# A four-layer streaming encoder step on one core: the residual stream kept transposed, with the output weights as the stationary operand

## The chip, the cores and the metric

The kernel runs on one core of a Trainium2 chip. The metric is the device time of one execution in microseconds, as the median of several executions. TensorE (PE) multiplies matrices; VectorE (DVE), ScalarE (ACT) and GpSimd (POOL) work element by element; SyncE (SP) issues the transfers (DMAs) between memory and the on-chip buffer.

## The reference

One inference step of an encoder with four layers (kinds A, B, C, A) over 512 prompt rows and 64 sample rows of width 1024. Every layer is

```
z = rmsnorm(x, norm_g) @ w_in          # one input projection: mixer inputs and a gate
o = mixer(z)                           # A, B, C: three kinds of attention with RMSNorm on q and k
x = x + (o * silu(gate)) @ w_out       # the residual

def rmsnorm(x, g):
    y = x * rsqrt(mean(x * x, axis=-1) + 1e-6)
    return y * g
```

In every mixer q and k pass through an RMSNorm per head; in kind C the low-rank q, the KV latent and the rotary key too. v and the gate don't.

## The kernel before

The 576 rows (TOK: 512 prompt, 64 sample) stand in five token tiles (TT): four of 128 and one of 64 rows. Widths of 1024 are cut into KD = 8 pieces of 128. All matmuls of the projections are made in a split form: each fp32 operand is written as a high part and a low part (fp32r), and a product is the sum of three matmuls, high by high, high by low and low by high. The high part is a copy on ACT, the low part a subtraction on DVE or POOL.

**Projections by token tile** (`mm_tok`, L155 to L175). The stationary operand (loaded into the array by a weight load of its own) is a 128x128 piece of the transposed activations (`xT` or `oT`), the moving operand a piece of the weights, up to 512 columns wide. The result has tokens on the partitions. The 64 sample rows put their high and low parts side by side as one 128-wide stationary operand (two matmuls in place of three), and the two halves of the result are added by ACT and DVE (`lo`).

**Gates** (`gates`, L211 to L236). Here the weights are stationary and the activations move, in two halves of 288 tokens (HALF): the result has the channels on the partitions and tokens on the free axis. One half gate is 8 x 3 matmuls, ACT's tanh, a DVE product, and in A and B a POOL product into the attention's output.

**Output projection** (`out_proj`, L257 to L265). Two halves of 512 output columns; in each, the five token tiles by `mm_tok`; a DVE addition onto the residual tile `x[t]`. In the second half `after` stores the tile to memory and calls `norm` for it.

**Norm and transposes** (`norm`, L184 to L202). For a token tile: square sum (ACT), power -0.5 (`rstd`: DVE, POOL), multiplication by the factor and by the gain row (DVE), eight transposes on PE through the identity, and the high and low parts of the next layer's `xT` (ACT, DVE).

**Splitting the operand** (`split_o`, L250 to L254). Eight blocks of the gated attention output: the high part on ACT, the low part on POOL as two instructions (512 and 64 columns).

**Order.** The program is written layer by layer, with units of projection work interleaved by hand into the attention (`mix`). The order on each engine is then made by a scheduler from the dependencies, and is fixed when the program is built. PSUM has eight banks: three for projections (tag `mm`), two for scores (`s`), two for transposes (`t`), one for attention outputs (`o`). Weights pass through four staging buffers (`ws`) and eight pairs of split ones (`wh`, `wl`).

Of the kernel before, what the change touches and what calls it, by code (L numbers as in the profile page):

```python
# [9 lines left out]
F32 = mybir.dt.float32  # L10
F32R = mybir.dt.float32r
# [29 lines left out]
def encoder_step(ctx: ExitStack, tc: tile.TileContext, I, O):  # L41
# [17 lines left out]

    def ps_s():  # L60
        return ps.tile([128, 512], F32, tag="s", name="s", bufs=2)
# [38 lines left out]
    x = []  # L100
# [3 lines left out]
    def load_x(pool, src):  # L104
        x.clear()
        for t, (t0, tn) in enumerate(TT):
            xt = sb(D, f"x{t}", pool=pool)
            last = ld(xt[:tn], src[t0 : t0 + tn, :])
            x.append(xt)
        return last.ins  # L110

    def rstd(ss, tn, n, inv):
        r = sb(n, "nv", pool=tiny)[:tn]
        for lo, hi, f in inv if isinstance(inv, list) else [(0, n, inv)]:
            V.tensor_scalar(out=r[:, lo:hi], in0=ss[:, lo:hi], scalar1=f, scalar2=EPS, op0=ALU.mult, op1=ALU.add)  # L115
        G.tensor_tensor(out=r, in0=r, in1=bc(mhalf[:tn], tn, n), op=ALU.pow)  # L116
        return r
# [36 lines left out]
    def mm_tok(xT, nh, t0, tn, pieces, n, p=None, c0=0, w0=0):  # L154
# [17 lines left out]
        lo = sb(512, "lo", 1)[:64, :n]  # L172
# [11 lines left out]
    def norm(t, g, xT):  # L184
        t0, tn = TT[t]
        ss = sb(1, "nss", pool=tiny)[:tn]
        junk = sb(D, "sq", 2, dt=BF16)[:tn]
        S.activation(junk, x[t][:tn], AF.Square, accum_out=ss)
        r = rstd(ss, tn, 1, 1.0 / D)
        for hf in range(2):  # L190
            xs = rows_of(tn)
            cs = slice(hf * 512, hf * 512 + 512)
            V.scalar_tensor_tensor(out=xs[:tn], in0=x[t][:tn, cs], scalar=r, in1=g[:tn, cs], op0=ALU.mult, op1=ALU.mult)  # L193
            pt = v3(ps_t(), 128)
            for j in range(4):
                tr(pt[:, j, :], xs[:, j * 128 : j * 128 + 128])
            k0 = hf * 4
            l0 = lo_at(t0, TOK)
            hl_evac(xT[:, k0 : k0 + 4, t0 : t0 + tn], xT[:, k0 : k0 + 4, l0 : l0 + tn], pt[:, :, :tn])
            if tn == DEC:  # L200
                end = V.tensor_copy(xT[:, k0 : k0 + 4, 2 * TOK : WT], xT[:, k0 : k0 + 4, TOK : TOK + DEC].bitcast(F32))
        return end.ins if tn == DEC else None  # L202
# [8 lines left out]
    def gates(xT, w, c0, ogs, done=None):  # L211
        st = []

        def half(m, og, hf):
# [35 lines left out]
    def split_o(oT, b, src):  # L250
        S.activation(oT[:, b, :TOK], src, AF.Copy)  # L251
        for a, c in ((0, SEQ), (SEQ, TOK)):
            l0 = lo_at(a, TOK)
            G.tensor_tensor(out=oT[:, b, l0 : l0 + c - a], in0=src[:, a:c], in1=oT[:, b, a:c].bitcast(F32), op=ALU.subtract)  # L254

    def out_proj(w, oT, after):
        for nh in range(2):  # L257
            pieces = load_chunk(w, [(nh * 512, 512)])
            for t in range(len(TT)):
                t0, tn = TT[t]  # L260
# [11 lines left out]
    def layer_a(li, xT, first=None):  # L272
        w = I["a_w_in"][li]
        with tc.tile_pool(name=f"la{li}", bufs=1, reuse_waits="tile") as lp:
# [4 lines left out]
            def v_units(pp, pieces=None):  # L279
                st = [pieces] if pieces else []  # L280

                def unit(t, t0, tn):
# [6 lines left out]
                    p = mm_tok(xT, TOK, t0, tn, st[0], 512)  # L289
                    S.activation(vt[:tn, t, :], p, AF.Copy)  # L290
# [4 lines left out]
            def qk_units(pr):  # L295
                st = []

                def unit(t, t0, tn):
# [10 lines left out]
                    r = rstd(ss, tn, 4, 1.0 / 128)  # L309
# [114 lines left out]
            run(u[1:])  # L424
            for p in range(4):
# [649 lines left out]
```

## Time and profile before

| what | value |
|---|---|
| median of 3 runs | 1267.1 us (1267.1 to 1268.33) |
| the profiled execution's own time | 1270.64 us |
| its span on the core | 1268.7 us |
| PE busy | 1239.4 us, 7479 matmuls |
| DVE, ACT, POOL busy | 717.2, 646.9, 383.6 us |
| share of PE in the chain that ended last | 94% |

The span is the time from the program's first instruction to its last on the core; the execution's own time has 1.94 us more around it. Busy times of PE count a matmul with its latency, so consecutive matmuls overlap in them: the rate at which PE works is read from the distance between starts, or from the busy time of a whole stretch over its count.

### The profile page before, as it was taken

To read this page: it belongs to the slowest core of one execution; us is meant where nothing else is said; L and a number is where in the kernel's file an instruction comes from. 1 tells how busy PE (TensorE), PEld (TensorE's weight loads), DVE (VectorE), ACT (ScalarE), POOL (GpSimd) and SP (SyncE) were. 2 spreads that over 40 slices of the span, in tenths; PEclk is the share of its full clock that TensorE was granted. 3 is DMA by queue.
4 is the path that set the end of the run, shared out by engine and by line. 5 is a ranking of instruction groups with operands and counts; after the bars stand their busy time and mean duration, and the time that the engine had idled before them with its cause. 6 is when DMAs were issued, how large, how long until landed. Compare 5 with 4: busy or idle time off the path is not lost.

```text
span 1268.7 us, 21162 instructions
## 1 busy us (share of the span) xinstructions
PE 1239.4 (98%) x7479; PEld 1064.4 (84%) x7479; DVE 717.2 (57%) x1975; ACT 646.9 (51%) x1637; POOL 383.6 (30%) x488
## 2 busy tenths in 40 slices
PE   6999999999999999999999999999999999999998
PEld 4888888998889999778998887876788888889986
DVE  5166534733669888526577767685263656247332
ACT  4345443652447676514466767686243454435431
POOL 3322202223145351321275444541310322022150
PEclk9999999999999999999999999999999999999999
DMA  6432341442446232334131111112344323424322
GB/s 208 131 94 88 105 142 51 141 141 72 164 118 214 58 90 61 125 100 134 58 100 52 53 30 34 35 51 71 101 163 140 95 89 102 131 62 143 111 78 69
DMA packets 92889, 127.12 MB, mean 100 GB/s; under 512 B 10864, under 2 KB 64528, under 8 KB 92720
## 3 DMA queue, kind: packets, MB, share of 16 engines
q1 hardware_dynamic: 92784, 125.77, 31.7%
q8 instruction: 59, 0.97, 0.3%
q14 instruction: 46, 0.38, 0.1%
HBM read 105.81 MB, written 24.26 MB: 103 GB/s over the span
## 4 chain that ended last, share of the span: by engine, by line
PE 94%; DVE 2%; ACT 2%; DMA 1%; issue 1%; SPq 0%; POOL 0%; DVEq 0%; POOLq 0%; ACTq 0%
PE mm L163 16%; PE mm L165 16%; PE mm L164 16%; PE t L178 9%; PE mm L224 5%; PE mm L225 5%; PE mm L226 5%; PE mm L168 4%; PE mm L169 4%; PE o L379 3%; PE s L856 3%; PE o L866 2%; PE s L371 2%; PE o L593 1%; DMA x<-in_x 1%
## 5 line engine op out<-in xcount | busy, mean ns | idle before, releaser
L116 POOL TENSOR_TENSOR nv<-nv,mhalf 128x4 f32<-128x4 f32 (+7 forms) x147 | 152.6, 1043 | 424.2 <-DVE nv L115 409.3
L120 ACT ACTIVATE wh<-ws 128x512 fp32r<-128x512 f32 (+2 forms) x288 | 169.4, 616 | 113.5 <-PE mm L168 73.2
L163 PE MATMUL mm<-wh,T 128*128 128x512 f32 (+2 forms) x608 | 222.4, 371 | 1.2 <-DVE qs L515 1.0
L165 PE MATMUL mm<-wh,T 128*128 128x512 f32 (+2 forms) x608 | 223.5, 369 | 0.0
L164 PE MATMUL mm<-wl,T 128*128 128x512 f32 (+2 forms) x608 | 220.8, 368 | 1.4 <-DVE wl L121 1.4
L121 DVE TENSOR_TENSOR wl<-ws,wh 128x512 fp32r<-128x512 f32 (+2 forms) x252 | 170.3, 697 | 36.5 <-ACT wh L120 33.0
L224 PE MATMUL mm<-T,wh 128*128 128x288 f32 x512 | 155.8, 304 | 0.1
L225 PE MATMUL mm<-T,wh 128*128 128x288 f32 x512 | 152.9, 299 | 0.0
L226 PE MATMUL mm<-T,wl 128*128 128x288 f32 x512 | 152.8, 299 | 0.0
L163 PEld LDWEIGHTS mm<-wh,T 128*128 128x128 f32 x608 | 114.9, 189 | 17.6 <-DVE qs L515 1.2
L164 PEld LDWEIGHTS mm<-wl,T 128*128 128x128 f32 x608 | 114.8, 189 | 17.5 <-DVE wl L121 1.8
L165 PEld LDWEIGHTS mm<-wh,T 128*128 128x128 f32 x608 | 114.8, 189 | 16.7 <-DVE T L182 0.6
L163 PE MATMUL mm<-wh,oT 128*128 128x512 f32 x256 | 99.7, 398 | 2.5 <-ACT oT L251 1.9
L165 PE MATMUL mm<-wh,oT 128*128 128x512 f32 x256 | 100.3, 399 | 1.3 <-POOL oT L254 1.3
L164 PE MATMUL mm<-wl,oT 128*128 128x512 f32 x256 | 100.9, 396 | 0.0
L224 PEld LDWEIGHTS mm<-T,wh 128*128 128x128 f32 x512 | 96.2, 188 | 3.4 <-issue 1.9
L225 PEld LDWEIGHTS mm<-T,wh 128*128 128x128 f32 x512 | 96.2, 188 | 1.9 <-issue 1.8
L226 PEld LDWEIGHTS mm<-T,wl 128*128 128x128 f32 x512 | 96.1, 188 | 1.1 <-issue 1.1
L232 POOL TENSOR_TENSOR o<-o,sq 128x288 f32<-128x288 f32 x52 | 44.8, 862 | 162.2 <-DVE sq L230 90.0
L263 DVE TENSOR_TENSOR x<-mm,x 128x512 f32<-128x512 f32 x32 | 21.6, 690 | 118.8 <-PE mm L165 113.9
L178 PE MATMUL t<-ident,qs 128*128 128x128 f32 (+1 forms) x376 | 62.1, 277 | 13.1 <-DVE qs L193 10.3
L349 DVE CUSTOM_DVE_ANT_0 ex<-s,bias 128x128 f32<-128x128 f32 (+1 forms) x64 | 30.9, 486 | 61.8 <-PE s L371 55.4
(256 smaller groups left out, 2665.6 us busy)
## 6 DMA issues: line engine op xcount, KB each, us to landing
ws<-in_a_w_in SPq DMA_DIRECT2D x64, 256.0 KB, 3.1
ws<-in_a_w_in SPq DMA_DIRECT2D x128, 128.0 KB, 2.3
ws<-in_b_w_in SPq DMA_DIRECT2D x40, 256.0 KB, 3.1
ws<-in_a_w_out SPq DMA_DIRECT2D x32, 256.0 KB, 3.9
xd<-x SPq DMA_DIRECT2D x12, 512.0 KB, 2.6
x<-xd SPq DMA_DIRECT2D x12, 512.0 KB, 5.5
ws<-in_c_w_in SPq DMA_DIRECT2D x24, 256.0 KB, 3.2
out_akT<-kf SPq DMA_DIRECT2D x8, 576.0 KB, 3.4
```

Source lines behind the costliest of these rows:

```text
L116: G.tensor_tensor(out=r, in0=r, in1=bc(mhalf[:tn], tn, n), op=ALU.pow)
L120: S.activation(h, src, AF.Copy)
L121: (eng or G).tensor_tensor(out=l, in0=src, in1=h.bitcast(F32), op=ALU.subtract)
L163: PE.matmul(out, xh, h[:, ws], start=(i == 0), stop=False)
L164: PE.matmul(out, xh, l[:, ws], start=False, stop=False)
L165: PE.matmul(out, xl, h[:, ws], start=False, stop=(i == last))
L168: PE.matmul(out, xs, h[:, ws], start=(i == 0), stop=False)
L169: PE.matmul(out, xs, l[:, ws], start=False, stop=(i == last))
L178: PE.transpose(out, in_, perm or ident)
L224: PE.matmul(p, wh, xT[:, k, cs], start=(k == 0), stop=False)
L225: PE.matmul(p, wh, xT[:, k, ls], start=False, stop=False)
L226: PE.matmul(p, wl, xT[:, k, cs], start=False, stop=(k == KD - 1))
```

## The change

The residual is kept as eight tiles of 128 channels by 576 tokens (`x0` to `x7`), both on the chip and in memory; the host passes the input transposed and transposes the output back.

- `out_proj` has the weights stationary, as the gates have: for each of eight blocks of 128 output channels and each half of 288 tokens, 8 x 3 matmuls. The results take turns in five banks (`ps_any`: three `mm`, two `s`). The sample rows have no form of their own there any more.
- `norm` and its transposes are gone. `feed` makes the high and low parts of `xT` straight from a residual tile, times the gain (now a number for each partition), without the norm's factor, and adds the squares into `acc`. `stats` then sums `acc` over the partitions by five small matmuls and takes the power. Where a head norm follows, the factor is left out and the head norm's epsilon is replaced by `ep`; v takes the factor as the scale of its evacuation (`rr`); the gates take it by a new DVE product with a row form of the factor (`rb`), which `spread` makes once per layer by two matmuls.
- `split_o` makes the low part in one instruction of 576 columns, on DVE for even blocks and on POOL for odd ones.
- The first projection of the first layer may use five banks as well.

```diff
+    def ps_any(i):
+        return ps_mm() if i % 5 < 3 else ps_s()
...
+    def feed(k, xk, g, xT, pool, eng, acc):
+        S.activation(xT[:, k, :TOK], xk, AF.Copy, scale=g[:, k : k + 1])
+        V.scalar_tensor_tensor(out=xT[:, k, TOK + DEC :], in0=xk, scalar=g[:, k : k + 1], in1=xT[:, k, :TOK].bitcast(F32),
+                               op0=ALU.mult, op1=ALU.subtract)
+        S.activation(xT[:, k, TOK : TOK + DEC], xT[:, k, 2 * TOK :].bitcast(F32), AF.Copy)
+        if k == 0:
+            S.activation(acc[:, :TOK], xk, AF.Square, scale=1.0 / 32)
+        else:
+            sq = sb(TOK, "xsq", 2, pool=pool)
+            S.activation(sq, xk, AF.Square, scale=1.0 / 32)
+            eng.tensor_tensor(out=acc[:, :TOK], in0=acc[:, :TOK], in1=sq, op=ALU.add)
+
+    def stats(pool, acc):
+        pt = ps_t()
+        for t in range(5):
+            PE.matmul(pt[:, 2 * t : 2 * t + 2], acc[:, 128 * t : 128 * t + 128], ones[:, 0:2], start=True, stop=True)
+        ve = sb(5, "ve", pool=tiny)
+        V.tensor_scalar(out=ve, in0=v3(pt[:, :10], 2)[:, :, 0], scalar1=EPS, scalar2=None, op0=ALU.add)
+        end = V.tensor_scalar(out=ep, in0=ve, scalar1=EPS, scalar2=None, op0=ALU.mult)
+        G.tensor_tensor(out=rr, in0=ve, in1=bc(mhalf, 128, 5), op=ALU.pow)
+
+    def spread():
+        for (a, b, ts) in ((0, SEQ, range(4)), (SEQ, TOK, (4,))):
+            dg = sb(512, "ex", 4)
+            for i, t in enumerate(ts):
+                V.tensor_scalar(out=dg[:, 128 * i : 128 * i + 128], in0=ident, scalar1=rr[:, t : t + 1], scalar2=None, op0=ALU.mult)
+            pb = ps_t()[:, : b - a]
+            PE.matmul(pb, ones, dg[:, : b - a], start=True, stop=True)
+            S.activation(rb[:, a:b], pb, AF.Copy)
...
-            th = sb(512, "sq", 2)[:, :HALF]
-            S.activation(th, p, AF.Tanh, scale=0.5)
+            V.tensor_tensor(out=z, in0=p, in1=rb[:, cs], op=ALU.mult)
+            S.activation(th, z, AF.Tanh, scale=0.5)
             g = th if done else og[:, cs]
-            V.scalar_tensor_tensor(out=g, in0=th, scalar=1.0, in1=p, op0=ALU.add, op1=ALU.mult)
+            V.scalar_tensor_tensor(out=g, in0=th, scalar=1.0, in1=z, op0=ALU.add, op1=ALU.mult)
...
-        for a, c in ((0, SEQ), (SEQ, TOK)):
-            l0 = lo_at(a, TOK)
-            G.tensor_tensor(out=oT[:, b, l0 : l0 + c - a], in0=src[:, a:c], in1=oT[:, b, a:c].bitcast(F32), op=ALU.subtract)
+        (V if b % 2 == 0 else G).tensor_tensor(out=oT[:, b, TOK:], in0=src, in1=oT[:, b, :TOK].bitcast(F32), op=ALU.subtract)
...
-    def out_proj(w, oT, after):
-        for nh in range(2):
-            pieces = load_chunk(w, [(nh * 512, 512)])
-            for t in range(len(TT)):
-                t0, tn = TT[t]
-                p = mm_tok(oT, TOK, t0, tn, pieces, 512)
-                xs = x[t][:tn, nh * 512 : nh * 512 + 512]
-                V.tensor_tensor(out=xs, in0=p, in1=xs, op=ALU.add)
-                after(t, nh)
+    def out_proj(w, oT, xs, after):
+        for pr in range(KD // 2):
+            pieces = load_packed(w, 256 * pr, 256)
+            for m in range(2):
+                db = 2 * pr + m
+                for hf in range(2):
+                    cs = slice(hf * HALF, hf * HALF + HALF)
+                    ls = slice(TOK + cs.start, TOK + cs.stop)
+                    p = ps_any(2 * db + hf)[:, :HALF]
+                    for k, (h, l) in enumerate(pieces):
+                        wh = h[:, m * 128 : m * 128 + 128]
+                        wl = l[:, m * 128 : m * 128 + 128]
+                        PE.matmul(p, wh, oT[:, k, cs], start=(k == 0), stop=False)
+                        PE.matmul(p, wh, oT[:, k, ls], start=False, stop=False)
+                        PE.matmul(p, wl, oT[:, k, cs], start=False, stop=(k == KD - 1))
+                    V.tensor_tensor(out=xs[db][:, cs], in0=p, in1=xs[db][:, cs], op=ALU.add)
+                    after(db, hf)
...
-            ld(xt[:tn], I["x"][t0 : t0 + tn, :])
-            x.append(xt)
-            if t == 0:
-                ld(ident, I["ident"])
-                nxt_gain = gain(xp, "a", 0)
...
+        load_gain(0)
+        for k in range(KD):
+            xk = sb(TOK, f"x{k}", pool=xp)
+            ld(xk, I["xT"][128 * k : 128 * k + 128, :])
+            first.append(load_w([I["a_w_in"][0][128 * k : 128 * k + 128, 2048:2560]], 512))
+            if k == 0:
+                acc = new_acc(xp)
+            feed(k, xk, gains[0], xT, xp, V, acc)
+        ld(ident, I["ident"])
+        end = stats(xp, acc)
```

Three places show how the order moves. The first is PE at the very start of the program, before the change (`T` is the operand `xT`, `qs` a normed token tile, `wh` and `wl` the weights of the first projection):

```order
L178 MATMUL t<-ident,qs 128x128 x8
L163 MATMUL mm<-wh,T 128x512
L164 MATMUL mm<-wl,T 128x512
L165 MATMUL mm<-wh,T 128x512
L163 MATMUL mm<-wh,T 128x512
L164 MATMUL mm<-wl,T 128x512
L165 MATMUL mm<-wh,T 128x512
L163 MATMUL mm<-wh,T 128x512
L178 MATMUL t<-ident,qs 128x128 x4
```

And PE at the same place in the changed program:

```order
L172 MATMUL mm<-wh,T 128x512 x3
L172 MATMUL s<-wh,T 128x512
L173 MATMUL mm<-wl,T 128x512
L174 MATMUL mm<-wh,T 128x512
L173 MATMUL mm<-wl,T 128x512
L174 MATMUL mm<-wh,T 128x512
L173 MATMUL mm<-wl,T 128x512
L174 MATMUL mm<-wh,T 128x512
L173 MATMUL s<-wl,T 128x512
L174 MATMUL s<-wh,T 128x512
L177 MATMUL s<-wh,T 128x512
L178 MATMUL s<-wl,T 128x512
```

No transposes stand there any more; the 14 matmuls of the first piece of the width, for all five token tiles, come first, in five banks.

The second place is PE at the boundary from the first layer to the second. In the changed program (L213 is `stats`; 37 matmuls of the next layer stand between the last one that reads `oT` and these five, and the first that reads the eighth piece of the new `xT` is the 29th of them):

```order
L174 MATMUL mm<-wh,T 128x512
L172 MATMUL mm<-wh,T 128x512
L213 MATMUL t<-ones,acc 128x2 x5
L173 MATMUL mm<-wl,T 128x512
L174 MATMUL mm<-wh,T 128x512
```

Before, groups of eight transposes stand among the same matmuls (here the last whole group of that boundary):

```order
L164 MATMUL mm<-wl,T 128x512
L165 MATMUL mm<-wh,T 128x512
L178 MATMUL t<-ident,qs 128x128 x8
L163 MATMUL mm<-wh,T 128x512
L164 MATMUL mm<-wl,T 128x512
```

What moved there: the transposes are gone, and a reduction stands once per boundary.

The third place is POOL ahead of the output projection of layer B, before (`o_3573`, `o_3574` are the attention's outputs, two blocks each):

```order
L232 TENSOR_TENSOR o_3576<-o_3576,sq 128x288 x3
L254 TENSOR_TENSOR oT<-o_3573,oT 128x512
L254 TENSOR_TENSOR oT<-o_3573,oT 128x64
L254 TENSOR_TENSOR oT<-o_3573,oT 128x512
L254 TENSOR_TENSOR oT<-o_3573,oT 128x64
L254 TENSOR_TENSOR oT<-o_3574,oT 128x512
L254 TENSOR_TENSOR oT<-o_3574,oT 128x64
```

And DVE at the same place in the changed program (POOL has four such instructions too):

```order
L279 TENSOR_TENSOR oT<-o_3660,oT 128x576
L254 TENSOR_TENSOR sq<-mm,rb 128x288
L279 TENSOR_TENSOR oT<-o_3661,oT 128x576
L279 TENSOR_TENSOR oT<-o_3662,oT 128x576
L257 SCALAR_TENSOR_TENSOR sq<-sq 128x288
L279 TENSOR_TENSOR oT<-o_3663,oT 128x576
```

Half of the blocks' low parts now stand on DVE, among the last gate's products, of which there is one more per half gate (L254).

## Rows read from the trace of the kernel before

**Rows 1.** The page: busy time by engine, and the chain that ended last.

```profile
PE 1239.4 (98%) x7479; PEld 1064.4 (84%) x7479; DVE 717.2 (57%) x1975; ACT 646.9 (51%) x1637; POOL 383.6 (30%) x488
...
PE 94%; DVE 2%; ACT 2%; DMA 1%; issue 1%; SPq 0%; POOL 0%; DVEq 0%; POOLq 0%; ACTq 0%
```

**Rows 2.** Windows of the four output projections, instructions on tile oT alone.

```profile
core 0: us, PE busy (x) PEld busy (x) ACT busy (x) POOL busy (x), PEclk, DMA share, GB/s
1210.80:1263.30 52.50, 52.44 (x224) 41.77 (x224) 1.38 (x2) 8.35 (x10) 1.00 0.25 83
286.40:340.70 54.30, 52.92 (x224) 41.62 (x224) 1.38 (x2) 8.34 (x10) 1.00 0.32 107
532.10:590.10 58.00, 55.01 (x224) 42.82 (x224) 4.13 (x8) 12.26 (x16) 0.97 0.43 142
887.50:942.60 55.10, 53.46 (x224) 41.66 (x224) 3.99 (x7) 12.29 (x16) 1.00 0.35 118
```

**Rows 3.** A window of gate matmuls, tile T alone; and PE's groups by form.

```profile
1204.10:1210.80 6.70, 6.66 (x50) 6.67 (x50) 0.00 (x0) 0.00 (x0) 1.00 0.22 73
...
L224 PE MATMUL mm<-T,wh 128*128 128x288 f32 x512 | 155.8, 304 | 0.1
L866 PE MATMUL o<-pa,v 128*64 128x512 f32 x32 | 17.2, 618 | 0.1
```

**Rows 4.** Timeline, first output projection (start, length); DVE groups of the norm.

```profile
330.33 0.39 PE L164 MATMUL mm<-wl,oT 128*128 128x512 f32 x1
330.56 1.03 PE L178 MATMUL t<-ident,qs 128*128 128x128 f32 x8
331.36 0.48 PE L165 MATMUL mm<-wh,oT 128*128 128x512 f32 x1
331.67 0.39 PE L163 MATMUL mm<-wh,oT 128*128 128x512 f32 x1
...
L193 DVE SCALAR_TENSOR_TENSOR qs<-x,nv,gain 128x512 f32<-128x512 f32 x32 | 24.4, 778 | 8.2 <-DMA gain<-in_a_norm 3.5 <-PE t L178 2.7 <-POOL nv L116 2.0
L193 DVE SCALAR_TENSOR_TENSOR half<-x,nv,gain 64x512 f32<-64x512 f32 x8 | 8.9, 1154 | 2.4 <-POOL nv L116 2.4
```

**Rows 5.** The start: timeline up to the second projection, and its window.

```profile
9.05 1.41 DVE L193 SCALAR_TENSOR_TENSOR qs<-x,nv,gain 128x512 f32<-128x512 f32 x2 [3.46 <-DMA gain<-in_a_norm]
9.85 1.97 PE L178 MATMUL t<-ident,qs 128*128 128x128 f32 x8 [9.85 <-DVE qs L193]
11.66 0.79 PE L163 MATMUL mm<-wh,T 128*128 128x512 f32 x1
45.51 0.61 PE L163 MATMUL mm<-wh,T 128*128 128x512 f32 x2
...
0.00:45.50 45.50, 33.59 (x152) 26.34 (x153) 20.71 (x36) 20.50 (x37) 13.50 (x22) 1.00 0.61 187
```

**Rows 6.** Timeline at layer B's output projection.

```profile
532.16 0.50 PE L163 MATMUL mm<-wh,oT 128*128 128x512 f32 x1 [1.01 <-ACT oT L251]
533.40 7.36 POOL L254 TENSOR_TENSOR oT<-o,oT 128x512 fp32r<-128x512 f32 x9
534.71 0.80 PE L165 MATMUL mm<-wh,oT 128*128 128x512 f32 x1 [1.34 <-POOL oT L254]
```

**Rows 7.** Timeline at the end of the program.

```profile
1263.33 0.59 ACT L173 ACTIVATE lo<-mm 64x512 f32<-64x512 f32 x1 [21.63 <-PE mm L169]
1264.67 0.68 DVE L263 TENSOR_TENSOR x<-lo,x 64x512 f32<-64x512 f32 x1
```

**Rows 8.** Windows of attention in layer B and layer C: PE, PEld, DVE, ACT, POOL busy.

```profile
400.00:520.00 120.00, 119.02 (x969) 111.24 (x968) 101.60 (x351) 84.69 (x266) 43.98 (x41) 1.00 0.26 77
660.00:880.00 220.00, 216.40 (x1448) 174.83 (x1446) 158.06 (x556) 159.28 (x464) 100.36 (x136) 1.00 0.15 42
```

**Rows 9.** DVE, ACT and POOL groups by form.

```profile
L230 DVE SCALAR_TENSOR_TENSOR sq<-sq,mm 128x288 f32<-128x288 f32 x52 | 23.4, 450 | 53.2 <-ACT sq L228 53.1
L251 ACT ACTIVATE oT<-o 128x576 fp32r<-128x576 f32 x32 | 19.6, 682 | 24.5 <-POOL o L232 24.5
L254 POOL TENSOR_TENSOR oT<-o,oT 128x512 fp32r<-128x512 f32 x32 | 42.4, 1324 | 9.1 <-ACT oT L251 9.1
```

More of the change, by code (lines that the diff above doesn't have):

```diff
@@ L98, in rows_of @@
         return half[turn[0]]
-    x = []
+    ones = sb(128, "ones", pool=const)
+    V.memset(ones, 1.0)
+    rb = sb(TOK, "rb", pool=const)
+    rr = sb(5, "rr", pool=const)
+    ep = sb(5, "ep", pool=const)
     late = [None]
@@ L104, in load_x, with rstd @@
     def load_x(pool, src):
[L105 to L108, printed above, removed]
-            x.append(xt)
-        return last.ins
-    def rstd(ss, tn, n, inv):
+        xs = []
+        for k in range(KD):
+            xk = sb(TOK, f"x{k}", pool=pool)
+            late[0] = ld(xk, src[128 * k : 128 * k + 128, :]).ins
+            xs.append(xk)
+        return xs
+    def rstd(ss, tn, n, inv, t=None):
         r = sb(n, "nv", pool=tiny)[:tn]
+        e = EPS if t is None else ep[:tn, t : t + 1]
         for lo, hi, f in inv if isinstance(inv, list) else [(0, n, inv)]:
-            V.tensor_scalar(out=r[:, lo:hi], in0=ss[:, lo:hi], scalar1=f, scalar2=EPS, op0=ALU.mult, op1=ALU.add)
+            V.tensor_scalar(out=r[:, lo:hi], in0=ss[:, lo:hi], scalar1=f, scalar2=e, op0=ALU.mult, op1=ALU.add)
         G.tensor_tensor(out=r, in0=r, in1=bc(mhalf[:tn], tn, n), op=ALU.pow)
@@ L182, in hl_evac, with new_acc @@
         V.tensor_tensor(out=dst_l, in0=src, in1=dst_h.bitcast(F32), op=ALU.subtract)
-    def norm(t, g, xT):
-        t0, tn = TT[t]
[L186 to L202, printed above, removed]
+    def new_acc(pool):
+        acc = sb(5 * 128, "acc", pool=pool)
+        V.memset(acc[:, TOK:], 1.0)
+        return acc
@@ L424, in layer_a @@
             run(u[1:])
+            spread()
             for p in range(4):
@@ L645, in layer_b @@
             run(q_units(0))
+            spread()
             weng[0] = G
@@ L890, in layer_c @@
             og, _ = og_tiles()
+            spread()
             qs_ = {}
@@ L908, in layer_c, with load_gain @@
         return og, lambda split: [u for b in CT for u in gate(b, done=lambda m: split(b))]
-    def gain(pool, nm, i):
-        g = sb(D, "gain", pool=pool)
-        ld(g, I[f"{nm}_norm"][i : i + 1].to_broadcast([128, D]))
-        return g
     layers = [("a", 0), ("b", 0), ("c", 0), ("a", 1)]
+    gains = []
+    for kind, li in layers:
+        gains.append(sb(KD, f"g{kind}{li}", pool=const))
+    def load_gain(i):
+        kind, li = layers[i]
+        ld(gains[i], I[f"{kind}_normT"][li])
     xT = big_xT()
@@ L936, in encoder_step @@
         with tc.issue_after(end):
+            for i in range(1, 4):
+                load_gain(i)
             for a, b, f in ((0, 2, 128 ** -0.5), (2, 3, 64 ** -0.5), (8, 32, -1.0)):
@@ L948, in encoder_step, with after @@
             ogs, tail = layer_c(xT)
-        x_new = dp.tile([TOK, D], F32, tag=f"xd{i}", name=f"xd{i}") if i < 3 else O["y"]
+        x_new = dp.tile([D, TOK], F32, tag=f"xd{i}", name=f"xd{i}") if i < 3 else O["yT"]
         nxt = {}
-        def after(t, nh):
-            t0, tn = TT[t]
-            if i == 3:
-                ld(x_new[t0 : t0 + tn, nh * 512 : nh * 512 + 512], x[t][:tn, nh * 512 : nh * 512 + 512])
-            elif nh == 1:
-                if "xT" not in nxt:
-                    nxt["xT"] = big_xT()
-                ld(x_new[t0 : t0 + tn], x[t][:tn])
-                norm(t, nxt_gain, nxt["xT"])
         with tc.tile_pool(name=f"op{i}", bufs=1, reuse_waits="tile") as op:
-            oT = v3(sb(KD * WT, "oT", dt=F32R, pool=op), WT)
+            oT = v3(sb(KD * 2 * TOK, "oT", dt=F32R, pool=op), 2 * TOK)
+            if i < 3:
+                acc = new_acc(op)
             def put(b):
                 split_o(oT, b, ogs[b])
+            def after(db, hf):
+                rows = slice(128 * db, 128 * db + 128)
+                if i == 3:
+                    cs = slice(hf * HALF, hf * HALF + HALF)
+                    ld(x_new[rows, cs], xs[db][:, cs])
+                elif hf == 1:
+                    if "xT" not in nxt:
+                        nxt["xT"] = big_xT()
+                    feed(db, xs[db], gains[i + 1], nxt["xT"], op, G, acc)
+                    ld(x_new[rows], xs[db])
             units = tail(put)
@@ L970, in encoder_step @@
             mix([lambda b=b: put(b) for b in range(KD) if b not in after_gate], units)
-            late[0] = load_x(op, x_src)
+            xs = load_x(op, x_src)
+            out_proj(I[f"{kind}_w_out"][li], oT, xs, after)
             if i < 3:
-                nxt_gain = gain(op, *layers[i + 1])
-            out_proj(I[f"{kind}_w_out"][li], oT, after)
+                stats(op, acc)
         x_src = x_new
@@ L979 @@
 _OUTS = {
-    "y": (TOK, D),
+    "yT": (D, TOK),
     "akT": (2, 8, 128, TOK),
```

49 lines of the change are left out of this document (23 added, 26 removed).

## The prediction

> **What bounds the kernel now.** I read the page first: PE is busy for 1239.4 of 1268.7 us, and PE holds 94% of the chain that ended last [rows 1]. So the time is, nearly everywhere, the number of matmuls times the distance at which PE starts them. That distance is not the length in the groups by form: a 288-column gate matmul is listed with 304 ns [rows 3], but a window with nothing else on PE has 50 of them in 6.66 us, 0.133 each [rows 3], and the fourth output projection 224 of 512 columns in 52.44 us, 0.234 each [rows 2]. What PE doesn't do, or waits for, then stands in three places: the start, where the first projection ends at 45.51 us [rows 5]; the output projections of B and C, which are longer than the fourth one [rows 2]; and DVE in layer B's attention, the only stretch where another engine is nearly full (101.60 of 120 us [rows 8]).
>
> **Output projection.** Per layer 224 matmuls at 0.234 (52.4 us) become 8 x 2 x 8 x 3 = 384 at 0.133 (51.1). Streams of gates are not all so clean, and the stage's edges cost the same as before; I take 0.8 off per layer of the 1.3, **-3.2 in all** (bounds -5.2 and 0). The gates are the very same instruction form, so this price is well known.
>
> Here a rule of the Trainium skill speaks against the change. The rows show 50 weight loads and 50 matmuls within the same 6.7 us, PEld busy all the while [rows 3], so loads run beside matmuls on the whole array. The Trainium skill, TensorE: Matmul & The Clock Gate, Part 3 (The mechanism), says that a weight load overlaps matmuls in flight only when it goes to other row groups, and the same page's section on LDWEIGHTS gives a load 107 ns for 128 columns. By that, as an estimate from that page, a 288-column matmul would take 0.227 us and one of 512 columns 0.320, and the four output projections 349 us after against 287 before. The trace disagrees at both widths (0.133 and 0.234), and the measurement decides.
>
> **Transposes of x.** The norm makes 32 + 8 half tiles on DVE [rows 4], four transposes each: 160, of which 40 belong to the start, below. Their price: from 330.33 to 331.67 PE starts two matmuls of 512 columns and eight transposes [rows 4]; 1.34 less 2 x 0.234 is 0.87, or 0.109 each. **120 x 0.109 = -13.1.** They stand in a full PE stream, so all of it counts.
>
> **Start.** Before, the first transposes begin at 9.85, after a wait of 3.46 us of DVE for the 512 KB gain row, the first projection matmul at 11.66, and the second projection at 45.51 [rows 5]. Changed, PE needs a small gain tile, 288 KB of x and 256 KB of weights; at the window's mean rate of 187 GB/s [rows 5] plus the lead of some 2 us that the first transfers need, that is 5 us, then a high part (0.68 [rows 9]) and the weights' low part on POOL (1.32 [rows 9]): first matmul near 7. From there 112 matmuls at 0.234 are 26.2, the five of `stats` 0.5, and early matmuls are slow: a length of 0.79 at 11.66 [rows 5] against 0.39 later [rows 4], as at the lower of the clock's two levels (1.2 of 2.4 GHz), though the window's granted clock reads 1.00 [rows 5]; twelve at double distance cost 2.8 us more. The end is near 36.5, and **-8.7** follows (the 40 transposes are in it). Data isn't late: 4.5 MB of x and weights at 187 GB/s are there by 26 us, when PE still has some 45 matmuls to make, and the order takes 14 per piece of the width. Bounds: -4 if the last pieces come 5 us late, -11 if PE starts at 5.
>
> **Boundaries of B and C.** B's stage is 58.0 us long, C's 55.1, the fourth 52.5 [rows 2]; less their 16 transposes (1.75), 3.75 and 0.85 are lost. In B PE waits 1.01 us for the high part and 1.34 for the low part, which POOL makes one by one in 7.36 us for nine instructions from 533.40 on [rows 6], after its gate products, and the window's granted clock is 0.97 [rows 2]: a dip from 2.4 to 1.2 GHz that costs 0.03 x 58 = 1.7 of the 3.75. In the change DVE makes the first low part at once, the two engines share the eight blocks, and PE has five banks' worth of first pieces. The wait for the high part stays. A gate's longer chain (one more DVE product) makes block 7 later by 0.45, against some 8 us of matmuls that stand ahead of it in the order. I take **-2.5**, from -4.6 (all of it) to +1.
>
> **The end.** After the last matmul the sample rows go through ACT's 0.59 from 1263.33 and two DVE instructions that end at 1265.35 [rows 7]. Changed, one DVE addition of 288 columns, 0.45 by its nearest form [rows 9]: **-1.5**.
>
> **What is added on PE.** Per layer five small matmuls (at most the transposes' 0.109 each), one fp32 matmul of 512 columns (no more than the listed length of one, 0.618 [rows 3]), one of 64 (0.109): 1.27, **+5.1** for four. Lower bound +3.
>
> **What is added elsewhere.** 64 DVE products at 0.45 [rows 9], 28.8 us; feeding, additions and half of the operand's split come to about what norm and its evacuations took. In A DVE has room, and so has C (158.06 of 220 us [rows 8]). In B's attention 12 products and the spread add 6.5 us to 101.60 of 120: 90%. What is queued behind a gate's product there is the softmax, and behind that PE. The bank is free after one DVE instruction where ACT and DVE were needed before. I take **+3** for B and C together, from 0 to +12: PE waits in these windows for only 1 and 3.6 us now [rows 8].
>
> POOL's squares and ACT's copies fit: per block of 128 channels PE works 6.4 us, ACT's feeding takes two of 0.68 and a short one, POOL's addition about 1.5 (576 columns at the rate of 1.32 for 512 [rows 9]). At the boundary the next layer needs the eighth piece after 28 matmuls, 6.5 us; from the last matmul an addition (0.45), a high part (0.68) and a low part (0.78 for 512 columns [rows 4], so 0.9) take 2.1, so 4 us are in hand. `stats` comes after 37 matmuls, 8.6 us, and its chain ends by about 5. Without that cover each of three boundaries would lose some 2 to 5 us.
>
> **Sum.** -3.2 - 13.1 - 8.7 - 2.5 - 1.5 + 5.1 + 3 = -20.9. The profiled execution, with its own time of 1270.64, becomes 1249.7. The median of the runs shown is 3.5 lower, 1267.1, and becomes 1246.2; I say 1246.5.
>
> **Rivals.**
> - *DVE takes a third of it back.* The new products delay the softmax in B and C, +10 to +12 where I took 3: 1255. For it: 90% busy in B, and a high share of DVE queues up in bursts. Against it: only 1 us of PE waits in B at 85% [rows 8].
> - *The boundary waits.* The next layer's first tile can't be finished before the eighth piece, where before it began on a finished tile. If ACT or DVE, with eight weight splits in their queues, is late by 4 us over the cover, `stats` stalls PE: 3 x 2.5 us, 1254. Against it: the weights of a pair fill half the buffers, so they are split ahead.
> - *The start stays.* If x and the weights come at a slower rate in more and smaller transfers, PE waits for pieces and ends its projection near 43: 1253.
> - *Slower by the products.* If every gate product stands wholly on PE's path, 28.8 where I took 3: 1272.3. It decides once 24 of the 28.8 us are exposed. Against it: in layers A, half of all gates, DVE is far from full, by the mean of 57% [rows 1].
> - *Weight loads exposed.* The change issues 640 more loads. If each cost the distance of a transpose, the closest row with a fresh load per 128 columns, they add 70 us: 1320. The skill's rule above is this rival, with an estimated 62 us more in the output projections; the gates' 0.133 [rows 3] leaves it little.
> - *No change*: the freed time turns into waits of PE elsewhere, 20 us of new ones: 1267.
>
> **Chances.** My forecast 0.68, DVE's third 0.10, boundary 0.08, start 0.06, products slower 0.03, loads 0.02, no change 0.03. Faster and slower count from 0.2%, 2.5 us, about what a measurement of this kernel can tell from no change. Faster 0.92, same 0.03, slower 0.05. The likeliest case has 1240 to 1254 by its bounds (start -11 and boundaries -4.6 below; DVE +8 and start -6 above). The range reaches up over the three partial cases: 1239 to 1258.
>
> **What would show it.** No transposes of x on PE and the second projection starting near 36 to 38 us; four output projections of 384 matmuls in 51 to 52 us each, B's no more than 2 us longer; `stats` and the matmuls of `spread` with no idle time before them; DVE at some 90% in B's attention with PE's waits there under 3 us. I am wrong if gate-like matmuls in the output projection start farther apart than 0.14, if PE idles before the eighth piece, or if the softmax groups of B and C show new waits of several us.

## The result, and the profile after

The changed kernel takes 1262.27 us (median of 7 runs, 1259.89 to 1264.76), the kernel before on the same chip 1268.26 (7 runs, 1267.10 to 1272.44). The ratio is 0.995, 95% interval 0.9937 to 0.9963: half a per cent faster, 6 us where 20.9 were forecast, and above the upper end of the range, 1258. The profiled execution took 1262.59 with a span of 1260.8.

The page of the changed kernel, busy time by engine and the chain that ended last, beside [rows 1]:

```profile
PE 1229.1 (97%) x8015; PEld 1097.0 (87%) x8015; DVE 756.0 (60%) x2031; ACT 659.0 (52%) x1653; POOL 392.3 (31%) x449
...
PE 89%; DVE 5%; POOL 2%; ACT 2%; issue 2%; DMA 1%; SPq 0%; DVEq 0%; POOLq 0%; ACTq 0%
```

PE has 10 us less to do, but a part of the chain has moved from PE (94 to 89%) to DVE (2 to 5%): something waits on DVE that did not wait before. Windows of the four output projections, instructions on tile oT alone, beside [rows 2] (busy times of PE, PEld, DVE, ACT and POOL, then PE's granted clock):

```profile
279.10:330.80 51.70, 51.35 (x384) 50.92 (x384) 0.75 (x1) 1.38 (x2) 1.78 (x2) 1.00 0.39 123
533.50:587.00 53.50, 52.96 (x384) 52.48 (x384) 5.40 (x4) 4.25 (x8) 7.00 (x4) 0.97 0.45 146
887.50:939.00 51.50, 51.42 (x384) 50.96 (x384) 6.34 (x4) 3.97 (x7) 7.28 (x4) 1.00 0.38 125
1205.90:1257.60 51.70, 51.34 (x384) 50.95 (x384) 0.75 (x1) 1.37 (x2) 1.81 (x2) 1.00 0.27 84
```

These are the 51 to 52 us that the prediction wanted, B's within the 2 us more that it allowed. The whole span, cut at the first and last matmuls that read `oT`, tells where the gain went (the forecast is the prediction's terms put where they belong: 16 transposes, 1.7 us, in each of the first three output projections and 24, 2.6 us, in each of the last three stretches of the layers, 1.27 of added PE work in every layer, half of the +3 in B and half in C):

| stretch | before | after | difference | forecast |
|---|---|---|---|---|
| start and first A, to its output projection | 286.5 | 279.1 | -7.3 | -7.4 |
| the four output projections | 219.6 | 208.0 | -11.6 | -10.9 |
| B | 191.5 | 202.8 | **+11.3** | +0.2 |
| C | 297.4 | 300.6 | **+3.2** | +0.2 |
| second A | 268.3 | 267.0 | -1.3 | -1.3 |
| after the last matmul | 5.4 | 3.2 | -2.2 | -1.5 |

So the stage that was rebuilt did as forecast, and layer B gave most of it back. The longest waits of PE before, from the first output projection to the second (who waited for whom, us in total, times, longest):

```profile
PE mm L163 <- DVE qs L515: 1.0, 1, 1.0
PE t L178 <- DVE qs L515: 1.0, 1, 1.0
```

And those of the whole changed kernel, of which the first and the last stand at the start of the program:

```profile
PE mm L172 <- ACT wh L129: 7.5, 1, 7.5
PE s L594 <- DVE nm L600: 5.9, 2, 5.4
PE mm L172 <- DVE hl L183: 3.4, 2, 3.1
PE t L213 <- DVE acc L208: 1.5, 1, 1.5
```

Two waits of B are new, those for `hl` and for `nm`. The first stands in the key projection. Timeline of the changed kernel, the rows about tile `hl`, and PE's first ones after the wait (start, length, idle time before with its releaser):

```profile
362.14 0.73 DVE L529 TENSOR_SCALAR hl<-t,par 64x512 f32<-64x512 f32 x1
...
363.21 0.64 SPq L530 DMA_DIRECT2D out_bkT<-hl  x1
...
366.54 0.59 ACT L182 ACTIVATE hl<-mm 64x512 f32<-64x512 f32 x1 [1.86 <-DMA out_bkT<-hl]
367.17 0.68 DVE L183 TENSOR_TENSOR hl<-mm,hl 64x512 f32<-64x512 f32 x1 [4.29 <-ACT hl L182]
...
368.00 0.55 PE L172 MATMUL mm<-wh,T 128*128 128x256 f32 x1 [3.09 <-DVE hl L183]
```

The diff also moved `mm_tok`'s sum of the sample rows from a buffer of its own (`lo`) into the tag (a named buffer that several tiles take in turn) `hl`, which has one buffer and from which B stages its keys for the store to `out_bkT`. The sum cannot start until that transfer has read the buffer, and PE, which waits for the sum, stands still for 3.1 us. The second wait is in the attention. DVE, POOL and PE of the changed kernel there:

```profile
418.84 4.93 DVE L607 TENSOR_SCALAR ex<-ex,ri 128x128 f32<-128x128 f32 x4
423.81 0.48 DVE L600 CUSTOM_DVE_ANT_0 ex<-s,bb,der 128x256 f32<-128x256 f32 x1
...
418.76 4.93 POOL L130 TENSOR_TENSOR wl<-ws,wh 128x512 fp32r<-128x512 f32 x4
...
424.76 0.58 PE L594 MATMUL s<-k,q 128*128 128x256 f32 x1 [5.39 <-DVE nm L600]
```

Four scalings of the softmax on DVE (L607), the shortest of which takes 0.27 us elsewhere, take 4.93, exactly as long as the four low parts of weights that POOL makes beside them. The score reduction (L600) stands behind them, and PE behind that. All 64 scalings of B, before and then in the changed kernel (busy us, mean ns of one):

```profile
L573 DVE TENSOR_SCALAR ex<-ex,ri 128x256 f32<-128x256 f32 x48 | 16.1, 396 | 0.3
L573 DVE TENSOR_SCALAR ex<-ex,ri 128x128 f32<-128x128 f32 x16 | 3.8, 283 | 0.2
```

```profile
L607 DVE TENSOR_SCALAR ex<-ex,ri 128x256 f32<-128x256 f32 x48 | 20.2, 482 | 0.3
L607 DVE TENSOR_SCALAR ex<-ex,ri 128x128 f32<-128x128 f32 x16 | 7.6, 532 | 0.1
```

After each of the two waits PE goes on at the lower of its clock's two levels, 1.2 of 2.4 GHz; windows of the changed kernel (behind the busy times of the five engines stands PE's granted clock):

```profile
368.00:371.40 3.40, 3.40 (x16) 3.40 (x17) 2.65 (x9) 1.36 (x4) 2.29 (x3) 0.50 0.18 54
422.60:429.40 6.80, 4.64 (x20) 2.65 (x20) 6.57 (x21) 3.25 (x11) 1.77 (x2) 0.50 0.36 113
```

Waits of 3.1 and 5.4, half of 3.4, and half of the 4.6 that PE works in the second window: 12.5 us in all, where B is 11.1 over its forecast.

### The profile page after: what moved, and what is told of

Its sections match the earlier page's. It is cut to its first block, busy times and chain, and to the rows that moved or that the text cites. A ratio compares the mean times of both kernels' runs of the same rounds, so it can differ in the third digit from the quotient of the medians.

```text
span 1260.8 us, 22340 instructions
## 1 busy us (share of the span) xinstructions
PE 1229.1 (97%) x8015; PEld 1097.0 (87%) x8015; DVE 756.0 (60%) x2031; ACT 659.0 (52%) x1653; POOL 392.3 (31%) x449
## 4 chain that ended last, share of the span: by engine, by line
PE 89%; DVE 5%; POOL 2%; ACT 2%; issue 2%; DMA 1%; SPq 0%; DVEq 0%; POOLq 0%; ACTq 0%
PE mm L174 10%; PE mm L173 10%; PE mm L172 10%; PE t L187 8%; PE mm L249 5%; PE mm L250 5%; PE mm L251 5%; PE mm L294 3%; PE mm L295 3%; PE mm L293 3%; PE o L412 3%; PE s L891 3%; PE mm L177 2%; PE mm L178 2%; PE o L901 2%; PE s L295 2%
## 5 line engine op out<-in xcount | busy, mean ns | idle before, releaser
L125 POOL TENSOR_TENSOR nv<-nv,mhalf 128x4 f32<-128x4 f32 (+6 forms) x127 | 139.0, 1101 | 323.1 <-DVE nv L124 276.6
L172 PE MATMUL mm<-wh,T 128*128 128x512 f32 (+2 forms) x600 | 217.3, 372 | 10.6 <-ACT wh L129 7.5
L174 PE MATMUL mm<-wh,T 128*128 128x512 f32 (+2 forms) x600 | 218.9, 368 | 0.0
L129 ACT ACTIVATE wh<-ws 128x512 fp32r<-128x512 f32 (+2 forms) x288 | 169.6, 615 | 68.1 <-PE mm L294 27.3
L130 DVE TENSOR_TENSOR wl<-ws,wh 128x512 fp32r<-128x512 f32 (+2 forms) x248 | 169.6, 699 | 48.9 <-ACT wh L129 45.0
L294 PE MATMUL mm<-oT,wh 128*128 128x288 f32 x320 | 94.7, 297 | 0.9 <-DVE oT L279 0.9
L293 PE MATMUL mm<-oT,wh 128*128 128x288 f32 x320 | 93.3, 297 | 1.9 <-ACT oT L278 1.9
L295 PE MATMUL mm<-oT,wl 128*128 128x288 f32 x320 | 94.0, 296 | 0.0
L208 POOL TENSOR_TENSOR acc<-acc,xsq 128x576 f32<-128x576 f32 x21 | 30.2, 1436 | 109.3 <-ACT xsq L207 109.3
L294 PEld LDWEIGHTS mm<-oT,wh 128*128 128x128 f32 x320 | 60.4, 189 | 1.8 <-DVE oT L279 1.8
```

What stands on the lines that cost most here:

```text
L129: S.activation(h, src, AF.Copy)
L130: (eng or G).tensor_tensor(out=l, in0=src, in1=h.bitcast(F32), op=ALU.subtract)
L172: PE.matmul(out, xh, h[:, ws], start=(i == 0), stop=False)
L174: PE.matmul(out, xl, h[:, ws], start=False, stop=(i == last))
L293: PE.matmul(p, wh, oT[:, k, cs], start=(k == 0), stop=False)
L294: PE.matmul(p, wh, oT[:, k, ls], start=False, stop=False)
```

## The experiments

Two theories for B: **the shared buffer** (the sum waits for the store of the keys) and **POOL holds DVE** (a run of POOL's low parts keeps DVE instructions that read and write the on-chip buffer at POOL's pace). The rivals are those of the prediction: DVE's load (the 64 new products), or the added PE work. All ratios are to the kernel before, on the same chip; the changed kernel stands at 0.995. Beside e1 to e4, e9 and e10 the kernel before has a median of 1269.0, beside e5 to e8, on another chip, 1268.15, so times of the two groups are compared to no better than 1 us.

**e1: the kernel before, with the shared buffer alone:**

```diff
-        lo = sb(512, "lo", 1)[:64, :n]
+        lo = sb(512, "hl", 1)[:64, :n]
```

> The kernel before with one thing of the change alone: the sample rows' summing buffer (lo) shares one buffer with the staging tile of layer B's keys (hl). Shared-buffer theory: in layer B's first projection ACT's copy of the sample rows waits for the keys' store to land, PE runs out of PSUM banks for about 3 us and the clock dips for 3.4 us, in all some 5 us: 1273 against 1268. Rival, that layer B's loss comes from DVE's added load: no change, 1268, and no wait of ACT on that store that reaches PE.

Measured: 1275.59 us, ratio 1.0055 (1.0042 to 1.0068). One line makes the kernel before 7 us slower, where 5 were expected, and the wait appears, of the same make:

```profile
375.55 0.64 SPq L496 DMA_DIRECT2D out_bkT<-hl  x1
378.80 0.59 ACT L173 ACTIVATE hl<-mm 64x512 f32<-64x512 f32 x1 [4.58 <-DMA out_bkT<-hl]
...
380.26 0.55 PE L163 MATMUL mm<-wh,T 128*128 128x256 f32 x1 [4.77 <-DVE hl L174]
```

**e2: the changed kernel, with a staging buffer of its own for the keys:**

```diff
-                    st = v3(sb(512, "hl", 1), 128)[:64, :, :tn]
+                    st = v3(sb(512, "bst", 1, pool=lp), 128)[:64, :, :tn]
```

> The changed kernel, but layer B's key staging for the store has a buffer of its own, so the sample rows' sum no longer shares one with it. Shared-buffer theory: the stall of 3.4 us at 364 us and the clock dip after it go, -4 to -5: 1257 to 1258 against 1262. The stall of 5.7 us at 419 us stays, if it is POOL's run of weight splits that blocks DVE there. Rival (DVE load): 1262, the same waiting elsewhere in B.

Measured: 1255.82, ratio 0.9903 (0.9887 to 0.9919). The wait on `hl` is gone from the list of waits, the one in the attention stays (5.1 us), with four scalings of 4.88 in all. B is 196.7 us long where it was 202.8. The shared buffer is shown from both sides, and costs some 6 to 7 us with the clock that falls behind it.

**e3: the changed kernel, with the low parts of the weights in B's attention made by DVE and POOL in turn** (`weng[0]` chose POOL for all of them):

```diff
-    turn = [0]
+    turn, wn = [0], [V, G]
+    flipped = lambda: (wn.reverse(), wn[0])[1]
...
-        split(h[:, :n], l[:, :n], w[:, :n], weng[0])
+        split(h[:, :n], l[:, :n], w[:, :n], weng[0] or flipped())
...
-            weng[0] = G
+            weng[0] = None
```

> The changed kernel, but the low parts of the weights during layer B's attention are made by DVE and POOL in turn where POOL made all. DVE gets 18 more instructions of 0.7 us, 13 us. Theory that a run of POOL subtractions holds DVE's on-chip instructions to POOL's pace (softmax scaling at 1.30 us each against 0.28): runs of four on POOL no longer exist, the stall of 5.7 us at 419 us and the 6.8 us of half clock after it shrink, -6 to -9: 1254. The stall at 364 us stays. Rival (DVE load): DVE is the full engine in B, 13 us more on it make the kernel slower, 1265 to 1270.

Measured: 1254.65, ratio 0.9889 (0.9876 to 0.9903). DVE has more to do here and is done sooner: the four scalings take 0.89, the wait ahead of the scores falls from 5.4 to 1.6, and the one on `hl` stays (2.7).

```profile
419.50 0.89 DVE L607 TENSOR_SCALAR ex<-ex,ri 128x128 f32<-128x128 f32 x4
```

**e4: both together** (the two edits above).

> Both edits, the keys' own staging buffer and the weight splits by turns in layer B. If both stalls are what the two theories say and independent: 1262 - 4.5 - 7.5 = 1250, near the 1246.5 that was forecast; B then takes some 190 us from the first to the second output projection's start less its own, against 202.8 now. Rival (DVE load): slower than e2 by up to 10 us.

Measured: 1251.13, ratio 0.9861 (0.9845 to 0.9877), better than either, and 11 us under the changed kernel; B takes 192.5 us. In this order two of POOL's low parts meet the scalings again, and the wait ahead of the scores is 3.2 us:

```profile
414.18 2.94 DVE L607 TENSOR_SCALAR ex<-ex,ri 128x128 f32<-128x128 f32 x4
...
414.33 2.50 POOL L130 TENSOR_TENSOR wl<-ws,wh 128x512 fp32r<-128x512 f32 x2
```

The runs that follow start from this kernel, "the repaired one".

**e5: the first layer's low parts on DVE too:**

```diff
-    weng[0] = G
+    weng[0] = V
```

> The repaired kernel (both repairs, 1251) with the first layer's weight low parts on DVE instead of POOL. If a run of POOL's splits is what holds DVE, the wait ahead of the first statistics (2.9 us at 24.1 in the repaired kernel) and the half-clock stretch behind it go, the second projection starts 2 to 4 us earlier, and the time is 1247 to 1249. If instead DVE's own load counts there, its 28 more splits of about 0.3 to 0.8 us delay the statistics and the time is 1252 to 1256.

Measured: 1250.05, ratio 0.9853 (0.9839 to 0.9866), by the medians not to be told from the repaired kernel, and between the two expectations. The place itself did as the theory said: the wait ahead of `stats` is gone, the second projection starts at 36.06 where it was 40.08, and the first output projection at 276.69 where it was 280.73. In the changed kernel DVE and POOL stood there as below, and in this one the same addition takes 0.75:

```profile
23.40 3.59 DVE L208 TENSOR_TENSOR acc<-acc,xsq 128x576 f32<-128x576 f32 x2
...
23.01 3.36 POOL L130 TENSOR_TENSOR wl<-ws,wh 128x512 fp32r<-128x512 f32 x2 [0.16 <-ACT wh L129]
```

```profile
20.89 0.75 DVE L208 TENSOR_TENSOR acc<-acc,xsq 128x576 f32<-128x576 f32 x1
```

Most of the 4 us was lost again later: in this profile PE is at half clock for 3.4 us in B's attention, in B's output projection and in C, where it is not in the profile of the repaired kernel, and B and C are 1.5 and 1.0 us longer.

**e9: all low parts of B's attention on DVE** (the kernel just told, and one line more):

```diff
-            weng[0] = None
+            weng[0] = V
```

> The kernel of e5 (both repairs and the first layer's splits on DVE, 1250) with layer B's attention making all its weights' low parts on DVE, none on POOL. If POOL's split is what holds DVE's scalings, the four scalings ahead of the scores at 411 us take about 0.28 us each again (2.94 us for the four in e5), their wait of PE shrinks from 3.2 us to about 2 or less though DVE now makes four splits of 0.68 there itself, and the time is 1247 to 1250. If DVE's load is what counts in B's attention, four splits more per group of four keep it longer than two, the wait there grows to 4 to 6 us, new ones of 1 us and more appear, and the time is 1253 to 1258.

Measured: 1249.18, ratio 0.985 (0.9835 to 0.9865), the fastest of the kernels that leave nothing out, though not apart from the last. This run decides between the theories: DVE makes every low part of B's attention itself, 24 instructions more from the first output projection to the second, and is not busy for longer, 152.17 us against 152.60. Windows of that stretch, of the changed kernel and then of this one:

```profile
330.70:533.60 202.90, 192.70 (x1436) 176.44 (x1434) 152.60 (x478) 119.84 (x351) 71.95 (x68) 0.97 0.27 78
```

```profile
327.80:520.10 192.30, 188.44 (x1435) 173.65 (x1434) 152.17 (x502) 119.25 (x351) 41.71 (x44) 1.00 0.28 83
```

The scalings take 17.8 us in all, where they took 27.8 in the changed kernel and 19.9 before:

```profile
L607 DVE TENSOR_SCALAR ex<-ex,ri 128x256 f32<-128x256 f32 x48 | 14.2, 359 | 0.1
L607 DVE TENSOR_SCALAR ex<-ex,ri 128x128 f32<-128x128 f32 x16 | 3.6, 284 | 0.2
```

The wait ahead of the scores is down to this:

```profile
PE s L594 <- DVE nm L600: 1.5, 2, 0.9
```

**e6: the repaired kernel without the gates' new product.** It leaves out the multiplication of the gates by the norm's factor:

```diff
-            V.tensor_tensor(out=z, in0=p, in1=rb[:, cs], op=ALU.mult)
-            S.activation(th, z, AF.Tanh, scale=0.5)
+            S.activation(th, p, AF.Tanh, scale=0.5)
...
-            V.scalar_tensor_tensor(out=g, in0=th, scalar=1.0, in1=z, op0=ALU.add, op1=ALU.mult)
+            V.scalar_tensor_tensor(out=g, in0=th, scalar=1.0, in1=p, op0=ALU.add, op1=ALU.mult)
```

> The repaired kernel without the 64 DVE products of the gates by the norm's factor; that leaves a part of the computation out (the gates go unnormalised), so its time only prices those products. My reading (hidden beside PE all but for the attention of B and C, where DVE is in demand): 1247 to 1250, the wait ahead of the scores at 415 us shorter by 1 to 3 us. The rival of the prediction, DVE takes back a third, 10 us or more: 1241 or less. Entirely hidden: 1250 to 1252.

Measured: 1252.71, ratio 0.9872 (0.9858 to 0.9885): not faster at all, above the 1250 that my own reading allowed and just above the 1252 for "entirely hidden". The rival by which the products take a third of the gain (1241) falls. C is shorter by 1.9 us (297.8 against 299.7), without PE's wait of 1.0 for the product; the wait ahead of the scores in B is the same 3.2 us, so it does not hang on the products. The granted clock of its runs is lower, as below.

**e7: without `spread` as well** (its three calls removed, the same part left out).

> The repaired kernel without the gate products and without the matmuls that spread the norm's factor over the partitions (the same part of the computation left out, and the factor's copies too); it prices the spread. Two fp32 matmuls per layer, by the trace of the changed kernel about 1.0 and 0.2 us of PE, four layers: 4 to 5 us less than without the products alone. By the prediction's price, 0.62 + 0.11 per layer: 2.9 less. If PE makes them in time that it would have waited in anyway: less than 1.

Measured: 1249.32, ratio 0.9849 (0.9835 to 0.9863), 3.4 us under the run before: between the 2.9 of the prediction's price and the 4 to 5 of the trace's. The second A, in which neither profile shows a fall of the clock, is 266.1 us long against 267.1, so one layer's `spread` costs 1.0.

**e8: all eight low parts of the operand on POOL again** (from the repaired kernel):

```diff
-        (V if b % 2 == 0 else G).tensor_tensor(out=oT[:, b, TOK:], in0=src, in1=oT[:, b, :TOK].bitcast(F32), op=ALU.subtract)
+        G.tensor_tensor(out=oT[:, b, TOK:], in0=src, in1=oT[:, b, :TOK].bitcast(F32), op=ALU.subtract)
```

> The repaired kernel with all eight low parts of the output projection's operand on POOL, as in the kernel before, instead of four on each engine. If the two engines in parallel shorten the boundary, as the prediction had it, the output projections of B and C get 1 to 2 us longer each and the time is 1253 to 1256. If the five banks' worth of first pieces cover a later low part, and DVE's own part is slowed by POOL's anyway (1.5 to 2 us for what takes 0.8 alone), 1250 to 1252.

Measured: 1256.36, ratio 0.9898 (0.9883 to 0.9914), 5 us more, at the upper end of what the first reading said. Its mechanism is only in part to be seen: the output projections of B and C are 0.8 and 2.1 us longer in the profile, but each holds 3.4 us at half clock, 1.7 us lost, that the repaired kernel's don't. PE's waits for low parts in the four projections are 1.2 us, where they were 0.8. Busy time of the two engines, though, is not saved by sharing: POOL alone needs 48.9 us for the 32 low parts, POOL and DVE together 27.3 and 21.2. Groups by form, of this kernel and of the repaired one:

```profile
L279 POOL TENSOR_TENSOR oT<-o,oT 128x576 fp32r<-128x576 f32 x32 | 48.9, 1557 | 8.0 <-DMA x<-in_xT 2.8 <-DMA x<-xd 2.8 <-ACT oT L278 2.4
```

```profile
L279 POOL TENSOR_TENSOR oT<-o,oT 128x576 fp32r<-128x576 f32 x16 | 27.3, 1726 | 10.0 <-ACT oT L278 10.0
L279 DVE TENSOR_TENSOR oT<-o,oT 128x576 fp32r<-128x576 f32 x16 | 21.2, 1349 | 8.2 <-ACT oT L278 8.0
```

**e10: three banks in the output projection instead of five** (from the repaired kernel):

```diff
-                    p = ps_any(2 * db + hf)[:, :HALF]
+                    p = ps_mm()[:, :HALF]
```

> The repaired kernel (both repairs, 1251) with the output projection's sums in the three banks of the ordinary matmul pool instead of five. If the five banks' first pieces are what keeps PE fed at the boundary, as the prediction had it, PE waits for the operand's last blocks at the start of each of the four projections and B's and C's get 1 to 3 us longer: 1254 to 1260. If three banks suffice, because the blocks come faster than 48 matmuls use them up, 1250 to 1252.

Measured: 1255.4, ratio 0.9896 (0.988 to 0.9913), 4 us more. The four projections are 0.3, 0.9, 0.9 and 0.3 us longer in the profiles (B's 53.7 against 52.8): 2.5 in all, less each than the 1 to 3 expected of B and C.

**The clock as a second account.** Each run lists its mean granted clock. At half speed half the time is lost, so (1 - clock) x span is what the clock cost that run, at most, since PE also waits in some of the slow stretches (a rounding of 0.0005 is 0.6 us). With that taken off:

| kernel | median | granted clock of its runs | time less that loss |
|---|---|---|---|
| changed | 1262.3 | 0.993, 0.992, 0.993, 0.996, 0.993, 0.995, 0.993 | 1253.3 to 1255.0 |
| repaired (e4) | 1251.1 | 0.998, 1.000, 1.000, 0.996 | 1248.1 to 1249.9 |
| start on DVE (e5) | 1250.1 | 0.996, 0.999, 0.999, 0.997, 0.996 | 1246.0 to 1247.9 |
| B on DVE too (e9) | 1249.2 | 0.999, 0.997, 1.000, 0.999 | 1246.5 to 1248.6 |
| no product (e6) | 1252.7 | 0.997, 0.994, 0.994, 0.995 | 1245.5 to 1246.6 |
| no product, no spread (e7) | 1249.3 | 0.997, 0.995, 0.996, 0.997 | 1243.8 to 1245.7 |
| split on POOL (e8) | 1256.4 | 0.993, 0.993, 0.993, 0.996 | 1247.3 to 1248.2 |
| three banks (e10) | 1255.4 | 0.996, 0.999, 0.997, 0.993, 0.995 | 1248.8 to 1252.0 |

Read so, the start is worth 1 to 2 us, the gate products 2 to 3, and `spread` 1 to 2, while the split on POOL costs nothing but clock. The changed kernel lost 5 to 10 us to the clock, and the runs of the kernel before, at 0.996 to 1.000, 5 at most. That the experiments' edits made the clock differ is not shown: a run's clock also differs from the next run's of the same kernel. Why the clock falls behind a wait in one run and not in another is not settled: the repaired kernel, e6 and e8 have the same wait of 3.2 us ahead of the scores, and in the profiles the clock falls behind it in the last two alone.

## Why the prediction was wrong

The step that failed is **"What is added elsewhere"**: +3 for B and C together, on the ground that feeding, additions and half of the split come to what they replace, with DVE's load as the only risk. B alone came out 11.1 over its forecast, for two reasons that the step does not have:

- **The shared buffer.** The prediction counts what the moved work costs and not where its results lie. The line is in the diff, and the trace of before has the store of the keys; what I left out was to ask who else uses the tag `hl`, and until when. Shown by e1 (it makes the wait alone) and e2 (without it the wait is gone).
- **POOL holds DVE.** I priced DVE by its busy share (90% in B) and POOL by its own list, as if the two didn't touch. The attention's new order sets four of POOL's low parts beside the four scalings; why the scheduler's order came out so stays open. Shown by e3, e5 and, with DVE's own load raised, by e9. Rivals about DVE's load fall with e6 and e9.

The other steps, in their order:

- *Output projection* (51.1 each) and *transposes*: right. The first and fourth projection are 51.35 and 51.34 us by the rows; there are no transposes of x.
- *Start*: the second projection starts at 38.49 where 36.5 was forecast, so the start gained 7.0 and not 8.7. That the stretch up to the first output projection holds (-7.3 against -7.4) is luck: its rest is 0.3 shorter where the added PE work was to make it longer. The working has two slips besides: 45.51 less 36.5 is 9.0, not 8.7, and the 0.5 of `stats` is counted here and once more in the +5.1; by its own rows the forecast gain was 0.8 too small. The first matmul starts at 7.47 (forecast: near 7). The 1.5 us of wait for `acc` is POOL holding DVE again; in e5, without it, the second projection starts at 36.06.
- *Boundaries*: B's output projection is 1.7 us longer than the fourth, within the 2 that were allowed. Three banks and the split on POOL each cost 4 to 5 us by the medians, so both parts of that step do matter: the banks by some 2.5 us of the projections, the split only with the clock, as far as these runs go.
- *The end*: -2.2 against -1.5. The tail is one DVE addition and the store:

```profile
1257.61 0.46 DVE L296 TENSOR_TENSOR x<-mm,x 128x288 f32<-128x288 f32 x1 [2.74 <-PE mm L295]
1258.09 0.33 SPq L1002 DMA_DIRECT2D out_yT<-x  x1
```

- *Added PE work*, 1.27 per layer: mis-sized. Each of the five small fp32 matmuls of `stats` stands as two records in the trace, ten in 1.17 us where 0.55 was taken; `spread`'s 512-column one too, and the next matmul but one starts 1.09 us after it, 0.86 more than the usual distance. With 0.2 for the 64 columns that is 2.2 per layer by these rows, 9 where 5.1 stood. The 1.0 for `spread` in the second A (e6 and e7) fits them; but the second A as a whole came out at its forecast of -1.3, so 0.9 was won there that no run explains. Timeline of the changed kernel:

```profile
339.00 1.17 PE L213 MATMUL t<-ones,acc 128*128 128x2 f32 x10
...
79.63 1.02 PE L226 MATMUL t<-ex,ones 128*128 128x512 f32 x2
80.09 0.79 PE L172 MATMUL mm<-wh,T 128*128 128x512 f32 x1
80.72 0.40 PE L173 MATMUL mm<-wl,T 128*128 128x512 f32 x1
```

- *DVE products*: some 2 to 3 of their 28.8 us by e6 once the clock is taken off, near what the step took; 1.9 of it in C, and in B's attention the wait ahead of the scores is the same without them.
- *Boundary waits, weight loads exposed*: neither came. `stats` waits for nothing at the three later boundaries.

With both faults mended (e4), the kernel is 17.9 us under the 1269.04 of before on that chip, and with the low parts of the start and of B's attention on DVE as well (e9) 19.8 under 1268.97, against the 20.9 of the sum. So the sum of the parts was nearly right, in part because its misses offset each other, and the two waits and the clock are what was missing. C's +3.2 is explained only in part: -2.6 for the transposes, +2.2 for `stats` and `spread` by the rows above, +1.9 for the products (e6), which is 1.5, and a stretch at half clock just ahead of its output projection. That stretch is worth 1.7 by its length, but the repaired kernel, which doesn't have it, is only 0.9 shorter in C (299.7), so 0.8 is left open. PE's waits for POOL's rotary products in C are 2.0 us where they were 0.5; the diff gives their temporaries one buffer instead of two, and no run tried that.

```profile
880.00:883.40 3.40, 3.40 (x8) 1.05 (x10) 0.00 (x0) 0.86 (x2) 0.00 (x0) 0.51 0.36 138
```

A buffer of its own for the sum itself wasn't tried; the keys' staging was moved instead.

## What to carry to other kernels

When a change renames a buffer or gives one away, list everyone who uses the new tag in the same stage, and when the last reader, a transfer above all, lets go of it: one line cost 7 us here. Price work on DVE with POOL's list beside it, not from its busy share: moving low parts from POOL to the busier DVE made DVE no busier (152.17 us against 152.60 in B) and the kernel faster. Where PE is nearly full, a wait costs its own length and, when the granted clock falls behind it, some 2 us more (3.4 us at half speed), so the experiments on short waits are read with the granted clock beside the time.

## What the hardware showed that I had not expected

- A DVE scaling that reads and writes on-chip memory takes 0.27 us alone and 1.30 beside POOL's subtractions of 512 columns, in step with them (four and four, 4.93 us each); an addition of 576 columns on DVE 0.75 alone and up to 1.85 beside them. DVE's addition onto the residual, which reads one operand from PSUM, keeps its 0.46 beside POOL's sums of the squares. The Trainium skill, SBUF — State Buffer, section Who interferes with whom, says that a DVE instruction of this kind can use a pair of ports that it shares with GpSimd, that the one which comes first keeps the pair for its whole length while the other waits, and that an addition with both inputs on-chip contends with a GpSimd instruction that reads on-chip memory as well. By that rule each scaling waits for the subtraction that came before it, and this trace agrees as far as its rows go: four scalings take as long as four subtractions (4.93 and 4.93).
- The split of the operand takes as much engine time on two engines as on one (48.5 against 48.9 us), perhaps for the same reason, which no run shows here; it gains only in that both work at once.
- A kernel without 64 DVE instructions of 0.45 us ran no faster (0.9872 against 0.9861); its runs were granted less clock (0.994 to 0.997 against 0.996 to 1.000). Why is not shown.
